# Loading the first gate block one step earlier, pairing rows of the narrow token blocks, other delays in a planner, and a last tile in halves

## The chip, the cores and the metric

One NeuronCore of a Trainium2 chip runs the whole program. The metric is the device time of one execution in microseconds; the median of three runs is given, and one further execution was taken with the profiler. TensorE (PE) does the matmuls, VectorE (DVE), ScalarE (ACT) and GpSimd (POOL) the element-wise work, SyncE (SP) issues the DMA transfers. Each engine works its own list of instructions in order, and waits where one of them needs another engine or a transfer.

## What is computed

One layer of an encoder: a normed input projection, differential attention and retention, and then the part that this change is in. 1024 prompt frames and 32 sample frames go through it together, 1056 tokens; the model has 1024 features, the feed-forward part 2816.

```python
def merge_and_tail(x, o_a, o_r, gate_a, gate_r, p, w_o, g_ffn, w_ff_gate, w_ff_up,
                   w_ff_down, g_ple, w_ple, w_ple_gate):
    mix = jax.nn.sigmoid(gate_a) * o_a + jax.nn.sigmoid(gate_r) * o_r
    x = x + mix @ w_o
    h = rmsnorm(x, g_ffn)
    x = x + (jax.nn.silu(h @ w_ff_gate) * (h @ w_ff_up)) @ w_ff_down
    gate = jax.nn.sigmoid(rmsnorm(x, g_ple) @ w_ple_gate)
    return x + gate * (p @ w_ple)
```

`rmsnorm` divides by the root of the mean square over the features and multiplies with a gain. The outputs are x for both sets of frames, and new keys, values and retention states.

## The kernel before

The matrices are fp32 and are multiplied as sums of 16-bit parts: every number is split into a high and a low half, and each product is three matmuls (L474, L475, L476: high-high, high-low, low-high). For that, each weight block comes by DMA into a stage buffer `st`, gets a scale, and is split into `w`.

Behind the attention stands one long stage, laid out by a planner (class `Flow`, L86). Each piece of work is a generator that yields what its next instruction costs and on which engine (`V`, `S`, `G`, `M` for VectorE, ScalarE, GpSimd, TensorE), waits for events, gets and puts buffers, or adds a `delay` to the time from which it may go on. The planner takes the piece that could start soonest by these estimates and writes out its instruction; so the estimates set the order of each engine's instructions, and where an operation may go on VectorE or GpSimd (`either_tt`, L1499) they choose the engine. Nothing of this runs on the chip: there only the resulting order exists.

The stage goes over the tokens in four blocks c0 to c3, of 352, 352, 176 and 176 tokens (`stream_bc`, L1796 on). For each block c and each of eight row tiles m (128 features), TensorE multiplies with w_o (24 matmuls to a tile). `residual(c)` (L1540) loads the block's x (`xf`, L1546), and for each m VectorE adds the product (L1553, the evacuation), SP stores the sum (L1556), ScalarE squares it (L1561), and VectorE adds the square to `acc` (L1564). TensorE then sums `acc` over the partitions (L1572, the norm sum of the block); VectorE, GpSimd and VectorE make of it `nbv`, `nbr` and `dg` (L1576, L1579, L1582), TensorE spreads `dg` (L1587), and VectorE scales the eight rows (L1591).

The gate and up projections follow in 22 weight blocks j. Two token blocks make a pair p: p = 0 is c0/c1, p = 1 is c2/c3; and (j, p) is gate block j on pair p, seven products of twelve matmuls. The pair's operands are not the rows themselves but rows and sums of rows: x1, x3, t1, t2, t4, x4 and t3. `sums(c, k)` (L1511) makes them by subtractions on VectorE or GpSimd, one row k at a time, and `parts16` (L1504) splits each into halves: ScalarE copies the high half (L1507), VectorE or GpSimd subtracts it to get the low half (L1501). x1, x3, t1 and x4 land in the tile called `mixs` in the trace, t2, t4 and t3 in `tT`.

`load_gu(j)` (L1613) brings a gate block: DMA into `st` (L1618, 1024 KB), two squares with a sum on ScalarE (L1630), their addition on VectorE (`wamh`, L1634), the sum over partitions on TensorE (L300, in `weight_scale`), a chain of tiny VectorE operations, and then seven splits shared by ScalarE, VectorE and GpSimd. The `delay` of L1635 tells the planner how long after `wamh` L300 is to be placed. Blocks 0 and 1 are asked for when the w_o loop reaches c = 1 (L1801), block 2 at c = 3, block 3 at (1, p = 0), and later blocks two steps ahead. There are two stage buffers.

The kernel's last stage (L1936 to L1960) goes over three blocks of 352 tokens and eight row tiles: 24 matmuls, a tanh on ScalarE (L1956), two VectorE operations (L1957, L1959) and a store (L1960).

Of the kernel before, what the change touches and what calls it, by code (L numbers as in the profile page):

```python
# [183 lines left out]
def kernel(  # L184
# [1278 lines left out]
    with ExitStack() as pc:  # L1463
# [18 lines left out]
        with ExitStack() as pw:  # L1482
# [20 lines left out]

            def parts16(key, out, src):  # L1504
                CW = WIDTH[2 * key[0]]
                yield S(CW, 0.05)
                nc.scalar.copy(out[0], src)  # L1507
                yield from either_tt(CW, out[1], src, out[0], ALU.subtract)
                yield ("set", ("o",) + key)

            def sums(c, k):  # L1511

                p, CW = c // 2, WIDTH[c]
                xa, xf, t = xfs[c - 1], xfs[c], tT[p]
                a1, a3, b2, b4 = xa[:, k], xa[:, HK + k], xf[:, k], xf[:, HK + k]
                cs = span(c)
                yield ("wait", ("o", p, "x1", k))
                yield from either_tt(CW, a1, b2, a1, ALU.subtract)
                flow.add(parts16((p, "t1", k), (xh1[:, k, 0, cs], xh1[:, k, 1, cs]), a1))

                if not p:
                    yield from either_tt(CW, b2, b4, b2, ALU.subtract)
# [4 lines left out]
                else:
                    yield ("wait", ("o", 0, "t2", k))
                    t2 = xfs[0][:, k, 0:CW]
                yield from either_tt(CW, t2, b4, a1, ALU.subtract)  # L1530
                flow.add(parts16((p, "t2", k), (t[:, T2, k, 0], t[:, T2, k, 1]), t2))
# [528 lines left out]
```

## Time and profile before

| | us |
|---|---|
| median of three runs | 1913.57 (1913.21 to 1913.68) |
| the profiled execution's own time | 1914.65 |
| its span, first to last instruction | 1912.8 |
| TensorE busy | 1860.5 (97%) |
| VectorE busy | 1503.2 (79%) |
| ScalarE busy | 1091.3 (57%) |
| GpSimd busy | 681.9 (36%) |

The mean granted clock of TensorE is 0.998 of full speed. The page gives these sums and the costliest groups of instructions; the views of the trace that are used below are the windows (how long each engine worked in a stretch, the granted clock there and the DMA engines' share), the waits (which instruction TensorE waited for, and how long), the timeline (single instructions, with the idle time ahead of them in brackets and what ended it), the instructions grouped by line and shape, and the DMA transfers with the time from issue to landing. Where neighbours of one line and shape follow each other, a timeline row holds several (x4), with the time from the first's start to the last's end. Matmuls overlap, so their spacing, not their length, is their price. The times of a trace count from its own start.

### The profile page before, as it was taken

The numbers are of one execution on the slowest core, as the hardware profiler recorded it, in microseconds if no ns is written. First come the engines' busy times: TensorE is split into PE (matmuls) and PEld (weight loads), VectorE is DVE, ScalarE is ACT, GpSimd is POOL, SyncE is SP. The second block draws the span as 40 slices with busy tenths as digits, with TensorE's granted clock in tenths as the row PEclk, the third lists the DMA queues.
The fourth block names the chain that finished last, engine by engine and source line by source line (L and its number), as shares of the span: only waits on it lengthen the run. The fifth ranks groups of instructions, "written<-read, shape, count | busy, mean of one in ns | idle before, by whom it ended". The sixth has DMA issues, their size and how long they took to land.

```text
span 1912.8 us, 38341 instructions
## 1 busy us (share of the span) xinstructions
PE 1860.5 (97%) x14183; PEld 1217.9 (64%) x14183; DVE 1503.2 (79%) x3955; ACT 1091.3 (57%) x2863; POOL 681.9 (36%) x1162
## 2 busy tenths in 40 slices
PE   7899999999999999999999998999999999999999
PEld 3556565555655566555556685777777776666665
DVE  7888888788787787777887589999999986654364
ACT  7777667677676776767656345655555552101132
POOL 3654444445444544544442067232232300000010
PEclk9999999999999999999999999999999999999999
DMA  5122112122021111211215610222111116112031
GB/s 192 71 72 78 60 32 82 36 57 81 26 68 58 50 64 34 80 59 30 85 34 191 222 65 29 101 83 87 65 59 63 50 53 262 62 61 79 11 133 50
DMA packets 71806, 146.91 MB, mean 77 GB/s; under 512 B 25249, under 2 KB 52001, under 8 KB 63682
## 3 DMA queue, kind: packets, MB, share of 16 engines
q1 hardware_dynamic: 71618, 144.46, 22.5%
q8 instruction: 111, 1.82, 0.4%
q14 instruction: 77, 0.63, 0.1%
HBM read 113.09 MB, written 31.34 MB: 76 GB/s over the span
## 4 chain that ended last, share of the span: by engine, by line
PE 70%; DVE 15%; POOL 6%; ACT 5%; issue 2%; DMA 1%; SPq 0%; POOLq 0%; ACTq 0%; DVEq 0%
PE ps L474 9%; PE ps L475 9%; PE ps L476 9%; PE pj L734 7%; PE pj L735 7%; PE pj L736 7%; PE ps L1478 4%; PE ps L1477 4%; PE ps L1476 4%; DVE nm L885 2%; ACT p L895 2%; DVE w L467 1%; POOL qkr L770 1%; PE sc L875 1%; PE sc L878 1%
## 5 line engine op out<-in xcount | busy, mean ns | idle before, releaser
L734 PE MATMUL pj<-w,xh 128*128 128x512 f16 x1024 | 388.9, 380 | 2.8 <-ACT w L465 2.8
L735 PE MATMUL pj<-w,xh 128*128 128x512 f16 x1024 | 389.0, 380 | 0.6 <-DVE w L467 0.6
L736 PE MATMUL pj<-w,xh 128*128 128x512 f16 x1024 | 389.0, 380 | 0.0
L475 PE MATMUL ps<-mixs,w 128*128 128x352 f16 (+1 forms) x960 | 260.6, 277 | 1.8 <-POOL mixs L1501 1.8
L474 PE MATMUL ps<-mixs,w 128*128 128x352 f16 (+1 forms) x960 | 260.7, 277 | 0.3 <-ACT pws L1354 0.3
L476 PE MATMUL ps<-mixs,w 128*128 128x352 f16 (+1 forms) x960 | 260.5, 277 | 0.0
L474 PEld LDWEIGHTS <-w 128*128 128x128 f16 x1728 | 169.7, 98 | 58.8 <-issue 5.1
L476 PEld LDWEIGHTS <-w 128*128 128x128 f16 x1728 | 169.5, 98 | 56.6 <-issue 5.6
L475 PEld LDWEIGHTS <-w 128*128 128x128 f16 x1728 | 169.5, 98 | 50.1 <-issue 1.3
L736 PEld LDWEIGHTS <-xh 128*128 128x128 f16 x1024 | 100.2, 98 | 122.3 <-issue 1.9
L1610 POOL TENSOR_TENSOR st<-st 128x512 f32<-128x512 f32 x66 | 86.2, 1305 | 250.7 <-DVE w L1605 186.6
L734 PEld LDWEIGHTS <-xh 128*128 128x128 f16 x1024 | 101.4, 99 | 76.7 <-issue 3.7
L735 PEld LDWEIGHTS <-xh 128*128 128x128 f16 x1024 | 100.2, 98 | 74.6 <-issue 3.7
L895 ACT ACTIVATE p<-sc,nb,scs 128x256 f32<-128x256 f32 (+7 forms) x128 | 106.6, 833 | 71.7 <-POOL nb L887 49.1
L475 PE MATMUL ps<-tT,w 128*128 128x352 f16 (+1 forms) x528 | 143.6, 277 | 3.5 <-DVE tT L1501 3.5
L476 PE MATMUL ps<-tT,w 128*128 128x352 f16 (+1 forms) x528 | 143.7, 277 | 0.0
L474 PE MATMUL ps<-tT,w 128*128 128x352 f16 (+1 forms) x528 | 143.6, 277 | 0.0
L1605 DVE SCALAR_TENSOR_TENSOR w<-st,gus,w 128x512 f16<-128x512 f32 x132 | 140.7, 1067 | 0.1
L885 DVE TENSOR_REDUCE nm<-sc 128x2 f32<-128x256 f32 (+6 forms) x112 | 102.9, 918 | 19.5 <-PE sc L878 18.3
L1478 PE MATMUL ps<-a,w 128*128 128x352 f16 x312 | 97.5, 313 | 0.5 <-DVE w L1696 0.5
L1476 PE MATMUL ps<-a,w 128*128 128x352 f16 x312 | 97.5, 313 | 0.0
L1477 PE MATMUL ps<-a,w 128*128 128x352 f16 x312 | 97.5, 312 | 0.0
(432 smaller groups left out, 4874.4 us busy)
## 6 DMA issues: line engine op xcount, KB each, us to landing
st<-in_win_dram SPq DMA_DIRECT2D x30, 1024.0 KB, 4.8
st<-in_wgu_dram SPq DMA_DIRECT2D x22, 1024.0 KB, 4.9
st<-in_wdn_dram SPq DMA_DIRECT2D x16, 704.0 KB, 4.5
out_dram<-kv SPq DMA_DIRECT2D x64, 128.0 KB, 1.7
a_d<-a SPq DMA_DIRECT2D x9, 528.0 KB, 2.6
b<-a_d SPq DMA_DIRECT2D x9, 528.0 KB, 7.1
mixs<-mix_d SPq DMA_DIRECT2D x8, 528.0 KB, 7.0
pw_d<-pws SPq DMA_DIRECT2D x12, 352.0 KB, 5.1
```

The costliest lines, as they stand in the source:

```text
L474: nc.tensor.matmul(out=ps, lhsT=wh, rhs=ah, start=first, stop=False)
L475: nc.tensor.matmul(out=ps, lhsT=wh, rhs=al, start=False, stop=False)
L476: nc.tensor.matmul(out=ps, lhsT=wl, rhs=ah, start=False, stop=last)
L734: nc.tensor.matmul(out=ps, lhsT=xhi, rhs=w[:, k, 0], start=(k == 0), stop=False)
L735: nc.tensor.matmul(out=ps, lhsT=xhi, rhs=w[:, k, 1], start=False, stop=False)
L736: nc.tensor.matmul(out=ps, lhsT=xh[:, k, 1, t0:t0 + P], rhs=w[:, k, 0], start=False, stop=(k == KD - 1))
L885: nc.vector.tensor_reduce(out=nm[0:R, mc], in_=pv, axis=AX.X, op=ALU.max, negate=True)
L895: nc.scalar.activation(pt[0:R, 0:NK], ps[0:R, p0:p0 + NK], AF.Exp, bias=nb[0:R, m:m + 1], scale=sc_ap[0:R], accum_out=Z[0:R, m:m + 1])
L1476: nc.tensor.matmul(out=ps, lhsT=wt[:, 0, j], rhs=a[:, 0, cs], start=(first and j == js[0]), stop=False)
L1477: nc.tensor.matmul(out=ps, lhsT=wt[:, 1, j], rhs=a[:, 0, cs], start=False, stop=False)
L1478: nc.tensor.matmul(out=ps, lhsT=wt[:, 2, j], rhs=a[:, 1, cs], start=False, stop=(last and j == js[-1]))
L1605: nc.vector.scalar_tensor_tensor(out=w[:, i, 1], in0=src, scalar=s, in1=w[:, i, 0], op0=ALU.mult, op1=ALU.subtract)
```

## The change

Four edits. (1) `load_gu(0)` is added when the w_o loop is at c = 0, and `load_gu(1)` at c = 1. (2) `ROWS = (1, 2)`: for the pair c2/c3, squares, `acc` additions, copies, subtractions and splits handle two rows of 176 in one instruction; the norm sum of c2 and c3 then takes eight small matmuls and no longer four. (3) The planner's delay behind `wamh` is 5.0 for the blocks 0 to 3 and stays 1.5 for the rest. (4) The last tile of the last stage is computed, evacuated and stored in two halves of 176 tokens.

```diff
@@ -1501,41 +1501,57 @@
                 ENG[g].tensor_tensor(out=out, in0=in0, in1=in1, op=op)
 
 
+
+            ROWS = (1, 2)
+
             def parts16(key, out, src):
-                CW = WIDTH[2 * key[0]]
-                yield S(CW, 0.05)
+                p, name, k = key
+                n, CW = ROWS[p], WIDTH[2 * p]
+                yield S(n * CW, 0.05)
                 nc.scalar.copy(out[0], src)
-                yield from either_tt(CW, out[1], src, out[0], ALU.subtract)
-                yield ("set", ("o",) + key)
+                yield from either_tt(n * CW, out[1], src, out[0], ALU.subtract)
+                for j in range(n):
+                    yield ("set", ("o", p, name, k + j))
 
             def sums(c, k):
 
                 p, CW = c // 2, WIDTH[c]
+                n = ROWS[p]
+                W = n * CW
+                lo, up = slice(k, k + n), slice(HK + k, HK + k + n)
                 xa, xf, t = xfs[c - 1], xfs[c], tT[p]
-                a1, a3, b2, b4 = xa[:, k], xa[:, HK + k], xf[:, k], xf[:, HK + k]
+                a1, a3, b2, b4 = xa[:, lo], xa[:, up], xf[:, lo], xf[:, up]
                 cs = span(c)
+
+                def row(ks):
+                    return xh1[:, ks, 0, cs], xh1[:, ks, 1, cs]
+
+                def tr(i):
+                    return t[:, i, lo, 0], t[:, i, lo, 1]
+
                 yield ("wait", ("o", p, "x1", k))
-                yield from either_tt(CW, a1, b2, a1, ALU.subtract)
-                flow.add(parts16((p, "t1", k), (xh1[:, k, 0, cs], xh1[:, k, 1, cs]), a1))
+                yield from either_tt(W, a1, b2, a1, ALU.subtract)
+                flow.add(parts16((p, "t1", k), row(lo), a1))
 
 ...
             def residual(c):
 
@@ -1546,7 +1562,8 @@
                 nc.sync.dma_start(out=xf, in_=xT[:, :, cs])
                 xfs.append(xf)
                 yield ("get", "acc")
-                acc = wkb.tile([P, CH], F32, tag="acc", name="acc")[:, 0:CW]
+                n = ROWS[p]
+                acc = wkb.tile([P, CH], F32, tag="acc", name="acc")[:, 0:n * CW]
                 for m in range(KD):
                     yield ("wait", ("wo", c, m))
                     yield V(CW, 1.0, 0.08)
@@ -1554,13 +1571,15 @@
                                                    op0=ALU.mult, op1=ALU.add)
                     yield ("put", "ps")
                     nc.sync.dma_start(out=x1_d[m, :, cs], in_=xf[:, m])
-                    if m:
+                    if m % n + 1 < n:
+                        continue
+                    if m >= n:
                         yield ("get", "sq")
-                    yield S(CW, 0.05)
-                    sq = wkb.tile([P, CH], F32, tag="sq", name="sq")[:, 0:CW] if m else acc
-                    nc.scalar.activation(sq, xf[:, m], AF.Square)
-                    if m:
-                        yield V(CW)
+                    yield S(n * CW, 0.05)
+                    sq = wkb.tile([P, CH], F32, tag="sq", name="sq")[:, 0:n * CW] if m >= n else acc
+                    nc.scalar.activation(sq.rearrange("p (a c) -> p a c", a=n), xf[:, m + 1 - n:m + 1], AF.Square)
+                    if m >= n:
+                        yield V(n * CW)
                         nc.vector.tensor_tensor(out=acc, in0=acc, in1=sq, op=ALU.add)
                         yield ("put", "sq")
                 yield ("get", "ss")
@@ -1569,8 +1588,9 @@
                 B = CW // 4
                 ps = pss.tile([P, 512], F32, tag="ss", name="ss")
                 for b in range(4):
-                    nc.tensor.matmul(out=ps[0:B, CW + b:CW + b + 1], lhsT=acc[:, b * B:(b + 1) * B], rhs=ones32[:, 0:1],
-                                     start=True, stop=True)
+                    for j in range(n):
+                        nc.tensor.matmul(out=ps[0:B, CW + b:CW + b + 1], lhsT=acc[:, j * CW + b * B:j * CW + (b + 1) * B],
+                                         rhs=ones32[:, 0:1], start=(j == 0), stop=(j + 1 == n))
                 yield V(4, 1.0, 0.1)
                 v = sm(4, "nbv")
                 nc.vector.tensor_scalar(out=v[0:B], in0=ps[0:B, CW:CW + 4], scalar1=_f(1.0 / D), scalar2=EPS, op0=ALU.mult, op1=ALU.add)
@@ -1590,8 +1610,12 @@
                     yield V(CW, 1.0, 0.08)
                     nc.vector.scalar_tensor_tensor(out=xf[:, k], in0=xf[:, k], scalar=gS[:, 1, k:k + 1], in1=ps[:, 0:CW],
                                                    op0=ALU.mult, op1=ALU.mult)
+                    k += 1 - n
+                    if k % n:
+                        continue
                     if not odd:
-                        flow.add(parts16((p, "x1" if k < HK else "x3", k % HK), (xh1[:, k, 0, cs], xh1[:, k, 1, cs]), xf[:, k]))
+                        ks = slice(k, k + n)
+                        flow.add(parts16((p, "x1" if k < HK else "x3", k % HK), (xh1[:, ks, 0, cs], xh1[:, ks, 1, cs]), xf[:, ks]))
                     elif k >= HK:
                         flow.add(sums(c, k - HK))
                 yield ("put", "ss")
@@ -1632,7 +1656,8 @@
                 yield V(1)
                 am = sm(1, "wamh", 3, BF16)
                 nc.vector.tensor_tensor(out=am, in0=am2[:, 0:1], in1=am2[:, 1:2], op=ALU.add)
-                yield ("delay", 1.5)
+
+                yield ("delay", 5.0 if j < 4 else 1.5)
                 s, d = yield from weight_scale(am, 1, 1, "gu", norm=True, total=True, at_bank=("ps", psb) if j < 4 else ("ss", pss))
 
                 yield V(1, 1.0, 0.2)
@@ -1798,9 +1823,8 @@
                 flow.add(residual(0), 0)
                 flow.add(residual(1), 0)
                 for c in range(NW):
-                    if c == 1:
-                        flow.add(load_gu(0), 2)
-                        flow.add(load_gu(1), 2)
+                    if c < 2:
+                        flow.add(load_gu(c), 2)
                     if c == 3:
                         flow.add(load_gu(2), 2)
                     if c in (1, 2):
@@ -1947,17 +1971,22 @@
                     norm2(wk, accs[c + 1], xts[c + 1], c + 1)
                 ms = slice(m % 4 * P, (m % 4 + 1) * P)
                 wt = wps[m // 4][0]
-                ps = bank()
-                for k in range(KD):
-                    xt = xts[c][k // 4][:, k % 4]
-                    mm3(ps, wt[:, k, 0, ms], wt[:, k, 1, ms], xt[:, 0], xt[:, 1], k == 0, k == KD - 1)
-                step()
-                th = wk.tile([P, CH], F32, tag="th", name="th")
-                nc.scalar.activation(th, ps, AF.Tanh, scale=hdp[:, m // 2:m // 2 + 1])
-                nc.vector.scalar_tensor_tensor(out=th, in0=th, scalar=1.0, in1=pws[:, m], op0=ALU.add, op1=ALU.mult)
-                yo = wk.tile([P, CH], F32, tag="yo", name="yo", bufs=3)
-                nc.vector.scalar_tensor_tensor(out=yo, in0=th, scalar=0.5, in1=x2[:, m, cs], op0=ALU.mult, op1=ALU.add)
-                nc.sync.dma_start(out=yT[m, :, cs], in_=yo)
+
+                n = 2 if (c, m) == (NCH - 1, KD - 1) else 1
+                for j in range(n):
+                    js = slice(j * CH // n, (j + 1) * CH // n)
+                    os = slice(cs.start + js.start, cs.start + js.stop)
+                    ps = bank()[:, 0:CH // n]
+                    for k in range(KD):
+                        xt = xts[c][k // 4][:, k % 4]
+                        mm3(ps, wt[:, k, 0, ms], wt[:, k, 1, ms], xt[:, 0, js], xt[:, 1, js], k == 0, k == KD - 1)
+                    step()
+                    th = wk.tile([P, CH], F32, tag="th", name="th")[:, js]
+                    nc.scalar.activation(th, ps, AF.Tanh, scale=hdp[:, m // 2:m // 2 + 1])
+                    nc.vector.scalar_tensor_tensor(out=th, in0=th, scalar=1.0, in1=pws[:, m, js], op0=ALU.add, op1=ALU.mult)
+                    yo = wk.tile([P, CH], F32, tag="yo", name="yo", bufs=3)[:, js]
+                    nc.vector.scalar_tensor_tensor(out=yo, in0=th, scalar=0.5, in1=x2[:, m, os], op0=ALU.mult, op1=ALU.add)
+                    nc.sync.dma_start(out=yT[m, :, os], in_=yo)
 
 
 # ---- launch: one core; inputs and outputs as the reference has them ----
```

What the change makes of the instructions' order. On SP, where the w_o loop begins, before (`xf` is x's load, `x_d` the store of the sum, `st` a weight block):

```order
L1546 DMA xf<-in_xT_dram 128x8x352 x2
L1556 DMA x_d<-xf 128x352 x2
L1546 DMA xf<-in_xT_dram 128x8x176
L1556 DMA x_d<-xf 128x352
L1618 DMA st<-in_wgu_dram 128x2048
```

The same place now, with the lines of the changed file:

```order
L1562 DMA xf<-in_xT_dram 128x8x352 x2
L1642 DMA st<-in_wgu_dram 128x2048
L1573 DMA x_d<-xf 128x352
L1562 DMA xf<-in_xT_dram 128x8x176 x2
L1573 DMA x_d<-xf 128x352
L1642 DMA st<-in_wgu_dram 128x2048
```

The first gate block's load moved ahead of the first stores, behind x's first two loads. On VectorE, in the same place, before:

```order
L461 SCALAR_TENSOR_TENSOR w<-st,wsk_16778,w 128x256 x4
L1553 SCALAR_TENSOR_TENSOR xf<-ps,o0d,xf 128x352
L461 SCALAR_TENSOR_TENSOR w<-st,wsk_16778,w 128x256 x3
L1553 SCALAR_TENSOR_TENSOR xf<-ps,o0d,xf 128x352
L461 SCALAR_TENSOR_TENSOR w<-st,wsk_16778,w 128x256
L1564 TENSOR_TENSOR acc<-acc,sq 128x352
```

And now:

```order
L461 SCALAR_TENSOR_TENSOR w<-st,wsk_16778,w 128x256 x4
L1570 SCALAR_TENSOR_TENSOR xf<-ps,o0d,xf 128x352
L461 SCALAR_TENSOR_TENSOR w<-st,wsk_16778,w 128x256 x3
L1570 SCALAR_TENSOR_TENSOR xf<-ps,o0d,xf 128x352
L1658 TENSOR_TENSOR wamh<-gam_16838 128x1
L461 SCALAR_TENSOR_TENSOR w<-st,wsk_16778,w 128x256
L1583 TENSOR_TENSOR acc<-acc,sq 128x352
```

`wamh` of gate block 0 came in ahead of w_o's last split; on TensorE its L300 stands behind the 96th of w_o's matmuls, where it stood behind the 264th. On TensorE, at the end of w_o on c3, where the first product of (0, p = 0) begins, before:

```order
L476 MATMUL ps<-mixs,w 128x176
L300 LDWEIGHTS cst_sb
L300 MATMUL mt<-wamh,cst_sb 128x1
L474 LDWEIGHTS w
L474 MATMUL ps<-mixs,w 128x352
```

24 matmuls of 352 columns later stood the norm sum of c3 (L1572). At that place now (L1592 is the norm sum):

```order
L476 MATMUL ps<-mixs,w 128x352
L1592 MATMUL ss<-cst_sb,acc 44x1 x8
L300 LDWEIGHTS cst_sb
L300 MATMUL mt<-wamh,cst_sb 128x1
L474 LDWEIGHTS w
L474 MATMUL ps<-mixs,w 128x352
```

Block 1's L300 moved from ahead of these 24 matmuls to behind the norm sum. In the same way block 3's L300, which stood inside (1, p = 1), now stands behind it and twelve matmuls of (2, p = 0); those of blocks 2 and 5 move by twelve matmuls. On VectorE, ahead of the norm sum of c3, before:

```order
L1564 TENSOR_TENSOR acc<-acc,sq 128x176
L1591 SCALAR_TENSOR_TENSOR xf<-xf,gS,ss 128x176
L1553 SCALAR_TENSOR_TENSOR xf<-ps,o1d,xf 128x176
L1591 SCALAR_TENSOR_TENSOR xf<-xf,gS,ss 128x176
L230 TENSOR_SCALAR guc<-mt 128x1
L1501 TENSOR_TENSOR mixs<-xf,mixs 128x176
L234 TENSOR_SCALAR gup_17938<-guc 128x1
L1501 TENSOR_TENSOR mixs<-xf,mixs 128x176
L1564 TENSOR_TENSOR acc<-acc,sq 128x176
```

And now:

```order
L1611 SCALAR_TENSOR_TENSOR xf<-xf,gS,ss 128x176 x3
L1570 SCALAR_TENSOR_TENSOR xf<-ps,o1d,xf 128x176
L1611 SCALAR_TENSOR_TENSOR xf<-xf,gS,ss 128x176
L1501 TENSOR_TENSOR tT_16818<-xf,tT_16818 128x352
L1583 TENSOR_TENSOR acc<-acc,sq 128x352
L1501 TENSOR_TENSOR tT_16818<-xf,tT_16818 128x352
L1501 TENSOR_TENSOR mixs<-xf,mixs 128x2x176 x2
```

The splits of x1 and x3 on c2 (`mixs`, 176) became pairs (2x176) and moved behind the last `acc` addition, which adds two rows. From VectorE's first subtraction (L1501) to that addition there are 36 instructions, before there were 43; up to the operands of (0, p = 1) 94, before 108. From about gate block 6 on, all engines have the same order as before, up to the last tile.

## Rows read from the trace of the kernel before

**Rows 1.** The page's first part: busy us, share of span, instructions.

```profile
PE 1860.5 (97%) x14183; PEld 1217.9 (64%) x14183; DVE 1503.2 (79%) x3955; ACT 1091.3 (57%) x2863; POOL 681.9 (36%) x1162
```

**Rows 2.** Windows: stretch, length; busy time (instructions) of PE, PEld, DVE, ACT, POOL; PEclk; DMA share; GB/s.

```profile
1054.40:1068.72 14.32, 14.32 (x97) 9.39 (x97) 8.79 (x25) 7.32 (x18) 0.00 (x0) 1.00 0.89 305
1054.40:1140.00 85.60, 85.60 (x748) 65.21 (x749) 57.22 (x115) 33.78 (x76) 29.02 (x27) 1.00 0.43 148
1140.00:1240.00 100.00, 84.35 (x728) 63.94 (x726) 98.28 (x216) 57.70 (x133) 55.37 (x57) 0.97 0.18 64
1148.00:1156.00 8.00, 5.97 (x36) 3.45 (x36) 8.00 (x24) 5.44 (x16) 6.77 (x8) 0.82 0.11 35
```

**Rows 3.** Waits of PE, 1085 to 1240: us in total, times, longest.

```profile
PE mt L300 <- DVE wamh L1634: 7.3, 5, 3.1
```

**Rows 4.** Timeline of PE: start, us, instruction, [idle before, releaser].

```profile
1148.03 0.16 PE L300 MATMUL mt<-wamh,cst_sb 128*128 128x1 bf16 x1 [3.07 <-DVE wamh L1634]
...
1155.16 0.46 PE L1572 MATMUL ss<-cst_sb,acc 128*44 128x1 f32 x8 [2.00 <-DVE gus L315]
...
1163.38 0.16 PE L300 MATMUL mt<-wamh,cst_sb 128*128 128x1 bf16 x1 [1.02 <-DVE wamh L1634]
...
1188.63 0.31 PE L475 MATMUL ps<-tT,w 128*128 128x176 f16 x1 [3.48 <-DVE tT L1501]
...
1193.04 0.24 PE L474 MATMUL ps<-mixs,w 128*128 128x176 f16 x1
...
1199.92 0.16 PE L300 MATMUL mt<-wamh,cst_sb 128*128 128x1 bf16 x1 [2.18 <-DVE wamh L1634]
```

**Rows 5.** Timeline of DVE, two places: w_o's splits, the last addition of c3.

```profile
1055.01 4.83 DVE L461 SCALAR_TENSOR_TENSOR w<-st,wsk,w 128x256 f16<-128x256 f32 x12
...
1153.62 1.40 DVE L1564 TENSOR_TENSOR acc<-acc,sq 128x176 f32<-128x176 f32 x1
```

**Rows 6.** Timeline of SP's queue: the loads of x for c0 and c1.

```profile
1054.83 1.85 SPq L1546 DMA_DIRECT2D xf<-in_xT_dram  x2
```

**Rows 7.** DMA issues of two short windows, c0's and c1's load: KB, us to landing.

```profile
xf<-in_xT_dram SPq DMA_DIRECT2D x1, 1408.0 KB, 9.6
...
xf<-in_xT_dram SPq DMA_DIRECT2D x1, 1408.0 KB, 12.2
```

**Rows 8.** Timeline of ACT: w_o's splits, and a gate block's squares.

```profile
1065.59 1.29 ACT L459 ACTIVATE w<-st,wsk 128x256 f16<-128x256 f32 x3
...
1087.84 1.04 ACT L1630 ACTIVATE w<-st 128x1024 bf16<-128x1024 f32 x1
...
1089.82 0.19 ACT L1630 ACTIVATION_READ_ACCUMULATOR w<-st 128x1 f32 x1
```

**Rows 9.** DVE by line and shape, 1131.8 to 1188.7: count | busy us, mean ns | idle.

```profile
L1501 DVE TENSOR_TENSOR tT<-xf,tT 128x352 f16<-128x352 f32 x8 | 5.5, 703 | 0.0
L1501 DVE TENSOR_TENSOR xf<-xf 128x352 f32<-128x352 f32 x6 | 5.5, 936 | 0.0
L1564 DVE TENSOR_TENSOR acc<-acc,sq 128x176 f32<-128x176 f32 x7 | 5.2, 739 | 0.0
L1501 DVE TENSOR_TENSOR mixs<-xf,mixs 128x176 f16<-128x176 f32 x6 | 4.5, 756 | 0.0
L1501 DVE TENSOR_TENSOR xf<-xf 128x176 f32<-128x176 f32 x4 | 2.9, 728 | 0.0
...
L1501 DVE TENSOR_TENSOR tT<-xf,tT 128x176 f16<-128x176 f32 x5 | 2.3, 484 | 0.0
...
L1501 DVE TENSOR_TENSOR mixs<-xf,mixs 128x352 f16<-128x352 f32 x1 | 1.2, 1168 | 0.0
```

**Rows 10.** Timeline of DVE: the last operation of the last tile.

```profile
1909.40 0.53 DVE L1959 SCALAR_TENSOR_TENSOR yo<-th,x 128x352 f32<-128x352 f32 x1
```

**Rows 11.** One line's instructions on DVE: duration ns min/median/max, first and last start, forms.

```profile
L1709 DVE SCALAR_TENSOR_TENSOR th<-th,snu x44: 328/432/835, 1173.4 to 1586.1; 128x352 f32<-128x352 f32 x22, 128x176 f32<-128x176 f32 x22
```

**Rows 12.** The page's DMA issues: KB each, median us to landing.

```profile
st<-in_wgu_dram SPq DMA_DIRECT2D x22, 1024.0 KB, 4.9
```

More of the change, by code (lines that the diff above doesn't have):

```diff
@@ L1527, in sums @@
                 else:
[L1528 to L1531, printed above, removed]
+                    for j in range(n):
+                        yield ("wait", ("o", 0, "t2", k + j))
+                    t2 = xfs[0][:, lo, 0:CW]
+                yield from either_tt(W, t2, b4, a1, ALU.subtract)
+                flow.add(parts16((p, "t2", k), tr(T2), t2))
                 yield ("wait", ("o", p, "x3", k))
-                yield from either_tt(CW, a3, t2, a3, ALU.subtract)
-                flow.add(parts16((p, "t4", k), (t[:, T4, k, 0], t[:, T4, k, 1]), a3))
+                yield from either_tt(W, a3, t2, a3, ALU.subtract)
+                flow.add(parts16((p, "t4", k), tr(T4), a3))
                 if p:
-                    flow.add(parts16((p, "x4", k), (xh1[:, HK + k, 0, cs], xh1[:, HK + k, 1, cs]), b4))
-                    yield from either_tt(CW, b2, b4, b2, ALU.subtract)
-                    flow.add(parts16((p, "t3", k), (t[:, T3, k, 0], t[:, T3, k, 1]), b2))
+                    flow.add(parts16((p, "x4", k), row(up), b4))
+                    yield from either_tt(W, b2, b4, b2, ALU.subtract)
+                    flow.add(parts16((p, "t3", k), tr(T3), b2))
             def residual(c):
@@ L1949 @@
                 wt = wps[m // 4][0]
-                ps = bank()
-                for k in range(KD):
-                    xt = xts[c][k // 4][:, k % 4]
-                    mm3(ps, wt[:, k, 0, ms], wt[:, k, 1, ms], xt[:, 0], xt[:, 1], k == 0, k == KD - 1)
-                step()
-                th = wk.tile([P, CH], F32, tag="th", name="th")
-                nc.scalar.activation(th, ps, AF.Tanh, scale=hdp[:, m // 2:m // 2 + 1])
-                nc.vector.scalar_tensor_tensor(out=th, in0=th, scalar=1.0, in1=pws[:, m], op0=ALU.add, op1=ALU.mult)
-                yo = wk.tile([P, CH], F32, tag="yo", name="yo", bufs=3)
-                nc.vector.scalar_tensor_tensor(out=yo, in0=th, scalar=0.5, in1=x2[:, m, cs], op0=ALU.mult, op1=ALU.add)
-                nc.sync.dma_start(out=yT[m, :, cs], in_=yo)
+                n = 2 if (c, m) == (NCH - 1, KD - 1) else 1
+                for j in range(n):
+                    js = slice(j * CH // n, (j + 1) * CH // n)
[11 more added lines that the diff above has]
+                    nc.sync.dma_start(out=yT[m, :, os], in_=yo)
 def _tables():
```

6 lines of the change are left out of this document (3 added, 3 removed).

## Prediction

> **What bounds the kernel now.** I read the page's busy shares first: TensorE works 97% of the span [rows 1]. So what can be won is the little time in which it stands still, and what can be lost is any new stand. The windows say where that is [rows 2]: from 1054.40, where w_o's matmuls begin, to 1140 it has no gap at all (85.60 of 85.60 us); from 1140 to 1240 it works 84.35 of 100 us, so 15.65 us stand open, and VectorE is busy 98.28 of these 100: VectorE paces there, and TensorE's waits are VectorE's queue. The waits of TensorE around that stretch name `wamh` five times, 7.3 us in all [rows 3]; this is the last VectorE step (L1634) before a gate block's scale goes through TensorE at L300. The timeline gives the places [rows 4]: 3.07 us at 1148.03 (block 1's scale), 2.00 at 1155.16 (norm sum of c3), 1.02 at 1163.38 (block 2's scale), 3.48 at 1188.63 (operands of block 0 on c2/c3), 2.18 at 1199.92 (block 3's scale).
>
> The clock is part of the price. From 1148 to 1156, right behind the 3.07 us wait, the granted clock is 0.82, while it is 1.00 where w_o runs [rows 2]: the lower of the two levels (1.2 instead of 2.4 GHz) took 0.18 x 8 = 1.4 us. The whole stretch from 1140 to 1240 has 0.97, that is 3 us, about two such falls, and it has two waits over 3 us. So I charge 1.4 us for a wait of over 3 us and nothing for one of about 2.
>
> **Part 1, gate block 0 asked for early.** Its load moves from the c == 1 step to c == 0. On SP it now stands directly behind the two `xf` loads. On TensorE its L300 stands behind 96 of w_o's matmuls and no longer behind 264; on ScalarE two squares go between w_o's last splits; on VectorE `wamh` goes ahead of w_o's last split and the evacuations behind it. When does TensorE ask, and when is it there?
> TensorE: 97 matmuls take 14.32 us from 1054.40 on, 0.148 each [rows 2]; the 96th ends at 1068.6.
> DMA: the stage buffer is the one that the first w_o block leaves. Its eighth split ends at 1055.01 + 8 x 0.40 = 1058.3 [rows 5]; from then on the transfer can be asked for. The two `xf` loads ahead, 1408 KB each, are issued from 1054.83 on, within 1.85 us [rows 6], the second 1.1 after the first; they take 9.6 and 12.2 us to land [rows 7], so they land at about 1064.4 and 1068.2, 3.8 us apart, with the DMA engines 0.89 busy [rows 2]. At that rate 1024 KB take 1024/1408 x 3.8 = 2.8 us: the block lands at about 1071.0.
> Then ScalarE squares the first half (1.04), does one w_o split (0.43), squares the second half (1.04) and reads the sum (0.19) [rows 8], and `wamh` follows: L300 can go at about 1071.0 + 2.7 = 1073.7. TensorE stands from 1068.6 to 1073.7, 5.1 us, and the clock falls: **+6.5 us**. At the window's mean of 305 GB/s [rows 2] the block takes 3.4 us, not 2.8, which makes 7.1; the bound below is that it doesn't queue at all, a rival below. Behind `wamh` VectorE's evacuations of w_o wait, behind the block x1's stores on SP's queue; TensorE wants neither before it goes on. Before the change block 0's L300 came without a wait. Nothing later takes the delay up: w_o runs without a gap to 1140, and the work that fills VectorE after that starts from products that are shifted with it.
>
> **Parts 2 and 3 up to the sum of c3** (times in before's frame, without part 1). `delay` 5.0 puts block 1's L300 behind the norm sum of c3. So the 3.07 us and their 1.4 go, and TensorE runs the 24 matmuls between the two places, from 1145.0 to about 1148.5, up to that sum. Now the accumulation of c3 is late instead. Before, its last add ran from 1153.62 for 1.40 us, to about 1155.0 [rows 5]. From its first subtraction at L1501 up to that add, VectorE now has 36 instructions where it had 43. By the mean of each form [rows 9]: out go 7 adds of 176 at 0.74, 3 `mixs` of 176 at 0.76, 2 `tT` of 352 at 0.70 and two tiny ones (5.2 + 2.3 + 1.4 + 0.1 = 9.0 us); in come 2 `xf` of 352 at 0.94, 2 `mixs` of 352 at 1.17 and 3 adds of 352. The stretch has no such add; the nearest rows are `tT` at 0.70 below and `mixs` at 1.17 above, and I take the 0.94 of `xf`, which also reads and writes fp32 (1.9 + 2.3 + 2.8 = 7.0). Net -2.0, bounds -1.3 and -2.7. The sum is free at about 1153.0; TensorE stands 4.5 us, and the clock falls. Against 1155.16 at full clock [rows 4] that leaves a gain of 0.7. Behind it the 1.02 us for block 2's scale goes, since its `wamh` now comes well ahead. So block 0 on c0/c1 ends about 1.7 us earlier.
>
> **Parts 2 and 3 on c2/c3.** Rows go two at a time there. TensorE wants the second pair of `t1` 19 matmuls into block 0 on c2/c3, and VectorE has to make it; before, its operands released TensorE last at 1188.63 [rows 4]. Over the whole piece, up to that point, VectorE has 94 instructions and had 108. By rows 9: adds -5.2 + 2.8; `mixs` of 176 -4.5, of 2x176 +2.8 (three at 0.94), of 352 +2.3; `tT` -2.4 (176) and -2.1 (352); `xf` of 176 -2.9, of 352 +2.8. Net -6.4; with each wide one that comes in at 1.17 it is -4.3, and VectorE may also have to wait for ScalarE's copies. So the pair is there between 1182.3 and 1185.5; I take 1184. TensorE, there since 1180, stands 4 us, loses 1.4 to the clock and has 65 matmuls of 176 left, which at half of 0.148 make 4.8: the block ends at 1190.3, where it was 1193.04 [rows 4]. That is -2.7 (bounds -1.2 and -4.5), and it contains the 1.7 above. Then block 1 on c2/c3 follows, and block 3's L300 now comes behind it and 12 more matmuls, later than its `wamh`: the 2.18 us go. Together **-4.9 us**, bounds -2.5 and -6.7. Blocks 2 and 5, whose places move by 12 matmuls, I set at nothing: what remains of the waits for scales, 7.3 less 3.07, 1.02 and 2.18 [rows 3, 4], is 1.0, and may double or go.
>
> Here the Trainium skill speaks against the merging. First the rows: VectorE's `xf` subtractions of 352 take 0.94 on average, those of 176 0.73 [rows 9], so twice the width costs 1.3 times the time. The Trainium skill's page "SBUF — State Buffer" (section "Who interferes with whom") says that a VectorE instruction with two SBUF inputs and a GpSimd instruction that reads SBUF exclude each other, and that the one which comes second is blocked for the whole of the other. By it a wide operation waits out a wide one of GpSimd, whose operations get wider too, and the sum would go towards the second rival's time.
>
> **Part 4, the last tile in two halves.** 48 matmuls of 176 cost what 24 of 352 did. Behind the last one, ScalarE's tanh and two VectorE operations of 0.53 each [rows 10] now work on half the columns. Such an operation took 0.33 at the least where half-wide ones ran [rows 11]: 2 x 0.2 us, and for the tanh and the half-sized store some 0.1 each: **-0.6 us**, bounds -0.3 and -0.9.
>
> **The sum.** +6.5 - 4.9 - 0.6 = +1.0 us on the profiled execution's own 1914.65, so 1915.7. That execution lies 1.08 above the median of 1913.57; against the median the forecast is **1914.6 us**. A measurement of this kernel can tell 0.2%, 3.8 us, from no change: faster means below 1909.7, slower above 1917.4.
>
> **Rivals.**
> *The early load needn't wait its turn (faster).* If the block doesn't stand behind `xf`, it needs what such a block needs in the median of all 22, 4.9 us [rows 12]: 1058.3 + 4.9 = 1063.2. ScalarE's squares are done by 1066, and TensorE never stands. From a landing before 1066 on the wait is nil: 1914.6 - 6.5 = 1908.1. A landing at 1068 leaves 2 us and no fall of the clock, 1910. Against it: the second `xf` landed 3.8 us after the first though issued 1.1 after it, so the queue worked them off one behind the other [rows 7]. For it: nothing but the median.
> *Wide operations eat the saving (slower).* Merged rows only pay while an operation of 352 costs less than two of 176. The one `mixs` of 352 took 1.17, two of 176 take 1.51 [rows 9], and GpSimd gets wide ones on the same tiles. If the wide ones average 1.4, as long as the add at 1153.62 took with 176 columns [rows 5], nine of them cost 0.4 to 0.5 more each, the pair comes at 1188, and the -2.7 turns to +1.2: the saving is gone and the new waits keep their falls of the clock. 1914.6 + 3.9 = 1918.5. It decides from about 1.35 us for a wide operation on.
> *Scales late again (near no change).* If block 3's `wamh` is late after all, 2.2 us come back: 1916.8. Another 1 to 2 us are possible where block 1's split weights, whose scale is now 5 us later, are wanted.
>
> **How the numbers follow.** The sum with its smaller variants (early wait 4.5 to 5.7, gate stretch within its bounds, a scale late): 0.63, times from 1911 to 1917.5. The early load without a wait or with a short one: 0.20, from 1905.5 to 1910.5. Wide operations eat the saving: 0.17, from 1917 to 1921. The range that leaves 2 in 10 out is 1907.5 to 1919. Faster: most of the second case and a little of the first, 0.24. Slower: most of the third and a little of the first, 0.22. Within: 0.54.
>
> **What would show it.** The changed kernel's TensorE must show one wait of 4.5 to 6 us at its first gate scale, behind w_o's 96th matmul, released by `wamh`, with a granted clock near 0.8 behind it; the first gate block landing 12 to 13 us after 1058; no wait at block 1's scale; one of about 4 us at the norm sum of c3; one of 3 to 5 us at a `mixs` of 176 in block 0 on c2/c3; none at block 3's scale; and the last store some 0.6 us sooner behind the last matmul. I am wrong if TensorE runs through the first scale, or if VectorE's mean for `xf` or `mixs` of 352 lies above 1.35 us.

## The result, and the profile after

The changed kernel takes 1918.61 us in the median of ten runs (1916.85 to 1920.16); the kernel before takes 1913.37 on the same chip. The ratio is 1.0026, with a 95% interval of 1.0018 to 1.0034: 5.2 us slower, more than the 0.2% that can be told from no change. The forecast was 1914.6 with "no change" as the likeliest; the time lies inside the range, 1907.5 to 1919, but only 0.4 us below its upper end. The profiled execution took 1918.57, its span is 1916.8, the mean granted clock 0.995.

The waits of TensorE from 1050 to 1260 (us in total, times, longest), where [rows 3] had five for `wamh`:

```profile
PE ps L475 <- DVE mixs L1501: 6.8, 1, 6.8
PE mt L300 <- DVE wamh L1658: 5.7, 1, 5.7
PE ss L1592 <- DVE acc L1583: 4.0, 1, 4.0
PE ss L1607 <- DVE dg L1602: 1.1, 1, 1.1
```

There are fewer waits, and they are longer: three over 3 us, before there were two. Their places, in TensorE's timeline (L1592 is the norm sum, L1658 `wamh`; the row at 1193.63 is the second pair of `t1`, that is its rows 2 and 3, which are made in one instruction now):

```profile
1053.52 0.31 PE L474 MATMUL ps<-mixs,w 128*128 128x352 f16 x1 [0.33 <-ACT pws L1354]
...
1067.69 0.31 PE L476 MATMUL ps<-mixs,w 128*128 128x352 f16 x1
1073.67 0.16 PE L300 MATMUL mt<-wamh,cst_sb 128*128 128x1 bf16 x1 [5.67 <-DVE wamh L1658]
...
1074.53 0.50 PE L474 MATMUL ps<-mixs,w 128*128 128x352 f16 x1
1074.83 0.50 PE L475 MATMUL ps<-mixs,w 128*128 128x352 f16 x1
...
1159.87 0.42 PE L1592 MATMUL ss<-cst_sb,acc 128*44 128x1 f32 x4 [3.99 <-DVE acc L1583]
...
1193.63 0.30 PE L475 MATMUL ps<-mixs,w 128*128 128x176 f16 x1 [6.75 <-DVE mixs L1501]
...
1201.34 0.24 PE L474 MATMUL ps<-mixs,w 128*128 128x176 f16 x1
...
1209.50 0.17 PE L300 MATMUL mt<-wamh,cst_sb 128*128 128x1 bf16 x1
```

The first gate scale stands behind w_o's 96th matmul (the row at 1067.69) and waits 5.67 us; the next matmuls are 0.30 apart. Block 3's scale at 1209.50 has no bracket: it doesn't wait any more. ScalarE's first square (L1654) tells when the block was there:

```profile
1070.06 1.06 ACT L1654 ACTIVATE w<-st 128x1024 bf16<-128x1024 f32 x1 [4.71 <-DMA st<-in_wgu_dram]
```

SP had asked for it at 1057.4, so it took 12.6 us to land, behind both loads of x; in this kernel's frame the forecast's 1071.0 is 1070.1. The windows behind the three long waits, and the stretch that [rows 2] showed (length; busy of PE, PEld, DVE, ACT, POOL; PEclk; DMA share; GB/s):

```profile
1073.67:1081.67 8.00, 8.00 (x46) 4.83 (x46) 7.18 (x18) 4.46 (x8) 1.94 (x2) 0.82 0.70 227
...
1159.87:1167.87 8.00, 8.00 (x47) 4.94 (x48) 6.64 (x18) 4.21 (x8) 5.25 (x4) 0.66 0.01 2
...
1193.63:1197.63 4.00, 4.00 (x28) 4.00 (x28) 3.96 (x7) 1.03 (x3) 1.75 (x2) 0.50 0.00 0
1197.63:1201.63 4.00, 4.00 (x43) 4.00 (x42) 4.00 (x12) 2.06 (x5) 0.04 (x1) 0.77 0.00 0
...
1140.00:1240.00 100.00, 88.19 (x768) 68.32 (x767) 95.65 (x191) 56.26 (x118) 60.08 (x50) 0.91 0.16 55
```

The lower clock costs (1 - 0.82) x 8 = 1.4 us behind the first wait, 0.34 x 8 = 2.7 behind the second and 0.50 x 4 + 0.23 x 4 = 2.9 behind the third. In the profile before, the same reckoning gave 1.4 at its first long wait.

So where did the time come from? Both kernels counted from their first w_o matmul (1054.40 and 1053.52; the 0.9 between them lies ahead of the change, and in the other runs' traces this matmul starts anywhere from 1053.2 to 1054.4):

| place | before | after | later by | forecast |
|---|---|---|---|---|
| norm sum of c0 | 1090.20 | 1096.57 | 7.2 | 6.5 |
| norm sum of c3, behind its wait | 1155.16 | 1159.87 | 5.6 | 4.5 |
| (0, c2/c3) begins | 1179.51 | 1185.28 | 6.6 | 4.8 |
| (1, c2/c3) begins | 1193.04 | 1201.34 | 9.2 | 3.8 |
| the next 352-column product, block 2 | 1201.77 | 1207.71 | 6.8 | 1.6 |
| two blocks on (their scales' waits gone too) | 1241.03 | 1245.59 | 5.4 | 1.6 |
| end of the span | 1912.8 | 1916.8 | 4.9 | 1.0 |

The early question (gate block 0 asked for one step sooner) cost about what it was to cost. Between the norm sum of c3 and the end of (0, c2/c3) the gain that was forecast didn't come.

### The profile page after: what moved, and what is told of

It is laid out like the page before. It is cut to its first block, busy times and chain, and to the rows that moved or that the text cites. A ratio compares the mean times of both kernels' runs of the same rounds, so it can differ in the third digit from the quotient of the medians.

```text
span 1916.8 us, 38364 instructions
## 1 busy us (share of the span) xinstructions
PE 1863.0 (97%) x14223; PEld 1221.7 (64%) x14223; DVE 1497.3 (78%) x3941; ACT 1087.9 (57%) x2842; POOL 676.9 (35%) x1148
## 4 chain that ended last, share of the span: by engine, by line
PE 72%; DVE 12%; POOL 7%; ACT 5%; issue 2%; DMA 2%; SPq 0%; POOLq 0%; ACTq 0%; DVEq 0%
PE ps L474 9%; PE ps L475 9%; PE ps L476 9%; PE pj L734 7%; PE pj L736 7%; PE pj L735 7%; PE ps L1478 4%; PE ps L1477 4%; PE ps L1476 4%; ACT p L895 2%; DVE nm L885 2%; DVE w L467 1%; POOL qkr L770 1%; PE sc L875 1%; PE sc L878 1%
```

## The experiments

Each was timed in five rounds against the kernel before on the same chip; the ratio is to that kernel, with its 95% interval, and the diffs are against the changed kernel unless something else is said.

| run | us | before, same chip | ratio |
|---|---|---|---|
| gate block 0 asked for late again | 1911.02 | 1913.57 | 0.9984 (0.9975 to 0.9993) |
| before, with the early question alone | 1925.25 | 1913.57 | 1.0059 (1.0047 to 1.0072) |
| single rows | 1917.63 | 1913.57 | 1.0020 (1.0011 to 1.0029) |
| early load, later scale | 1910.77 | 1913.57 | 0.9986 (0.9977 to 0.9994) |
| delays and tail only | 1910.89 | 1914.20 | 0.9984 (0.9975 to 0.9993) |
| pairing and tail only | 1910.50 | 1914.20 | 0.9982 (0.9973 to 0.9991) |
| no operand subtractions on GpSimd | 1925.80 | 1914.20 | 1.0060 (1.0048 to 1.0073) |
| norm sum of c3 later | 1919.32 | 1914.20 | 1.0027 (1.0017 to 1.0038) |
| block 0 ahead of c1's x | 1912.37 | 1913.84 | 0.9994 (0.9985 to 1.0003) |
| before, with the halved tail alone | 1913.32 | 1913.84 | 0.9998 (0.9989 to 1.0006) |
| early load, later scale, short delays | 1910.35 | 1913.84 | 0.9983 (0.9974 to 0.9992) |

### The early question

Undone:

```diff
-                    if c < 2:
-                        flow.add(load_gu(c), 2)
+                    if c == 1:
+                        flow.add(load_gu(0), 2)
+                        flow.add(load_gu(1), 2)
```

> The changed kernel with gate block 0 asked for at c == 1 again, together with block 1; paired rows, delays and the halved last tile stay. Theory (the early question makes TensorE stand 5.7 us behind w_o's 96th matmul and lose 1.4 us of clock, and gives nothing back): that wait is gone and the time falls by 7, to about 1911.4 (1910 to 1913). Rival (the early question also relieves VectorE in front of the gate blocks, since block 0's splits are done sooner): the waits at the norm sum of c3 (3.99) and at t1's second pair (6.75) grow by 2 to 4 us together, and the time is 1914 to 1916.

1911.02: 0.42% less than the changed kernel, 8 us. The waits at the norm sum and at t1's pair are what they were in the changed kernel:

```profile
PE ps L475 <- DVE mixs L1501: 6.7, 1, 6.7
PE ss L1592 <- DVE acc L1583: 4.0, 1, 4.0
```

So the early question gave nothing back behind its own wait; the rival, that it relieves VectorE later, falls. Done alone, in the kernel before (the same lines the other way round):

> The kernel before with gate block 0 asked for at c == 0 alone; the short delay then puts its L300 behind 72 of w_o's matmuls, 24 sooner than in the changed kernel. Theory: the block can't be there sooner, so TensorE stands 24 x 0.149 = 3.6 us longer than the 5.67 us there, some 9.2, and loses 1.4 us of clock: 1913.4 + 10.6 = 1924 (1922 to 1926). Rival (it relieves VectorE later): under 1920.

1925.25, 11.7 above before; its wait for `wamh` behind 72 of w_o's matmuls is 8.94 us. The block comes when it comes: a scale placed 24 matmuls sooner waits 3.3 us longer.

Is it the place in the queue that makes the block late? An exchange on SP's queue tells:

```diff
@@ residual(c), ahead of the load of xf
+                if c == 1:
+                    yield ("wait", "gu0")
@@ load_gu(j), behind its dma_start
+                if j == 0:
+                    yield ("set", "gu0")
```

> The changed kernel with one exchange on SP's queue: block 0's load goes ahead of the xf load of c1, behind that of c0 alone; all engines' orders stay. Theory (the block was late because 1408 KB of xf stood ahead of it in the queue): it lands some 3.5 us sooner, at about 1066.5 in the changed kernel's frame, wamh is there at about 1069.6, TensorE comes at 1068.0 and stands 1.6 us (0.5 to 2.5) in place of 5.67 and keeps its clock: 1918.6 - 4.1 - 1.4 = 1913.1 (1912 to 1914.5). Rival (the block's landing is set by the DMA engines' load and not by its place): as the changed kernel, 1917.5 to 1919.5.

1912.37, as the theory said. The block lands 8.7 us after its issue at 1057.1, at 1065.8, and in TensorE's timeline the wait is short and the matmuls behind it are 0.15 apart:

```profile
1069.44 0.16 PE L300 MATMUL mt<-wamh,cst_sb 128*128 128x1 bf16 x1 [1.75 <-DVE wamh L1662]
1069.46 0.31 PE L474 MATMUL ps<-mixs,w 128*128 128x352 f16 x1
1069.61 0.31 PE L475 MATMUL ps<-mixs,w 128*128 128x352 f16 x1
```

TensorE, VectorE, ScalarE and GpSimd have the orders of the changed kernel, so 6 us of its loss hang on SP's queue, and in the main on the 1408 KB of x that stood ahead of the block. A smaller thing moved with it: the loads of x for c2 and c3, issued from 1064.83 on in the changed kernel while the block was still landing, now come from 1069.72 on, when it is there. What they added to the 12.6 us isn't separated; the forecast of the landing, 1070.1, was met without them. The cheaper remedy leaves the queue alone and moves the scale:

```diff
-                yield ("delay", 5.0 if j < 4 else 1.5)
+                yield ("delay", 16.0 if j == 0 else 5.0 if j < 4 else 1.5)
```

> The changed kernel with a planner's delay of 16 behind the wamh of block 0 only: its L300 stands behind 168 of w_o's matmuls, where TensorE comes at about 1078.6, five us after wamh; the early load and squares stay. Theory: no wait and no fall of the clock at the first scale, the rest as in the changed kernel: 1918.6 - 7.1 = 1911.5 (1910 to 1913). Rival (the early load itself costs, by queueing in front of x1's stores or by splits among w_o's evacuations): 1914 to 1917.

1910.77. At 1078.60 TensorE runs through the first scale, and the rest is as it was: 4.0 at the norm sum, 6.7 at t1's pair.

### Pairing, delays and the tail

Single rows (`ROWS = (1, 1)`) in the changed kernel:

> The changed kernel with single rows on c2/c3 (ROWS of 1 and 1). Theory A (pairing rows saves VectorE some 3 us before t1's second pair): without it the waits at the norm sum and at t1 grow, 1920 to 1922. Theory B (pairing saves nothing, because GpSimd's wider operations hold VectorE up elsewhere by as much): within 1 us of the changed kernel, 1917.5 to 1919.5. Theory C (pairing is what makes t1 late): 1914 to 1916.

1917.63: theory B, pairing saves no time. But the waits are others. In this kernel they are (1055 to 1240):

```profile
PE ss L1592 <- DVE acc L1583: 5.5, 1, 5.5
PE mt L300 <- DVE wamh L1658: 4.9, 1, 4.9
PE ps L474 <- ACT w L1626: 2.8, 1, 2.8
PE ps L476 <- DVE w L1629: 2.5, 1, 2.5
```

At t1 there is none; TensorE now waits for block 1's split weights at (1, c0/c1), whose scale the delay moved back, and comes to (0, c2/c3) at 1194.0 when the operands are there. With pairs it comes at 1185.3 and waits to 1193.6. So pairs don't bring VectorE through any sooner: its last operand subtraction (L1501) starts at 1193.50 with pairs and at 1190.97 with single rows, GpSimd's last at 1194.25 and 1198.47.

The same without the early question, once with the delays and once with the pairing (the diffs are the lines above; the latter has `delay` 1.5 throughout):

> The changed kernel with gate block 0 asked for at c == 1 and with single rows: of the four edits only the delays and the halved last tile stay. Theory (pairing gives nothing in time, since GpSimd holds VectorE up elsewhere by as much): as e1_late_ask, 1911.0, within 1.2 us. Rival (pairing gave 2 us that the early question hid): 1912.5 to 1914.

> The changed kernel with gate block 0 asked for at c == 1 and the delay of 1.5 for all blocks: of the four edits only pairing and the halved last tile stay. Theory (the delays take away the waits at the scales, some 2.2 us in (1, c2/c3) and 0.9 at block 5, while VectorE sets the rest): 3 us slower than e1_late_ask, 1913 to 1915. Rival (VectorE sets everything up to block 6, delays don't matter): 1910.5 to 1912.

1910.89 and 1910.50, and both edits together 1911.02. In the first, theory as expected; in the second the rival, which said that the delays don't matter beside pairing. Either edit alone, with the tail, is worth 3 to 4 us, and the second adds nothing to the first. In the run with pairing and tail the scales of the blocks 3 and 5 don't wait either, though their delay is 1.5 as before, where they waited 2.18 and 0.91; the waits for the blocks 1 and 2 are still there, 2.50 and 1.02. The tail by itself:

> The kernel before with the last tile in halves, nothing else. Theory: 0.6 to 0.8 us less than before, since the last tanh, two VectorE operations and store work on half. Rival (twice the small matmuls and weight loads eat it): no change.

1913.32 against 1913.84, 0.5 less; the interval (0.9989 to 1.0006) doesn't exclude "no change". The traces show it more sharply: from the last matmul's start to the end of the span it is 1912.8 - 1907.9 = 4.9 us before, and 1916.8 - 1912.6 = 4.2 in the changed kernel, where the last operations are these:

```profile
1913.31 0.34 DVE L1986 SCALAR_TENSOR_TENSOR th<-th,pws 128x176 f32<-128x176 f32 x1 [1.10 <-ACT th L1985]
1913.69 0.34 DVE L1988 SCALAR_TENSOR_TENSOR yo<-th,x 128x176 f32<-128x176 f32 x1
```

### VectorE and GpSimd

What did pairing do to VectorE? By line and shape, in the changed kernel from 1137 to 1193.7 (count | busy us, mean ns), the lines that answer to [rows 9] and some others:

```profile
L1629 DVE SCALAR_TENSOR_TENSOR w<-st,gus,w 128x512 f16<-128x512 f32 x9 | 9.5, 1079 | 0.0
...
L1501 DVE TENSOR_TENSOR xf<-xf 128x352 f32<-128x352 f32 x9 | 5.5, 630 | 0.0
L1501 DVE TENSOR_TENSOR mixs<-xf,mixs 128x352 f16<-128x352 f32 x6 | 4.4, 741 | 0.0
L1501 DVE TENSOR_TENSOR tT<-xf,tT 128x352 f16<-128x352 f32 x6 | 4.2, 698 | 0.0
L1583 DVE TENSOR_TENSOR acc<-acc,sq 128x352 f32<-128x352 f32 x4 | 4.1, 1017 | 0.0
L1602 DVE TENSOR_TENSOR dg<-cst_sb,nbr 44x176 f32<-44x176 f32 x2 | 3.7, 1862 | 0.9 <-POOL nbr L1599 0.9
L1658 DVE TENSOR_TENSOR wamh<-gam 128x1 bf16<-128x1 f32 x2 | 3.0, 1478 | 0.0
...
L1739 DVE SCALAR_TENSOR_TENSOR a<-a,th 128x352 f16<-128x352 f16 x2 | 2.3, 1202 | 0.0
...
L1734 DVE SCALAR_TENSOR_TENSOR th<-th,snu 128x352 f32<-128x352 f32 x1 | 1.2, 1250 | 0.0
```

The same lines before, from 1131.8 to 1188.7, where [rows 9] doesn't show them:

```profile
L1605 DVE SCALAR_TENSOR_TENSOR w<-st,gus,w 128x512 f16<-128x512 f32 x9 | 8.2, 923 | 0.0
...
L1582 DVE TENSOR_TENSOR dg<-cst_sb,nbr 44x176 f32<-44x176 f32 x2 | 2.4, 1191 | 0.9 <-POOL nbr L1579 0.9
...
L1714 DVE SCALAR_TENSOR_TENSOR a<-a,th 128x352 f16<-128x352 f16 x2 | 1.7, 875 | 0.0
...
L1634 DVE TENSOR_TENSOR wamh<-gam 128x1 bf16<-128x1 f32 x2 | 1.4, 682 | 0.0
...
L1709 DVE SCALAR_TENSOR_TENSOR th<-th,snu 128x352 f32<-128x352 f32 x1 | 0.8, 835 | 0.0
```

The wide subtractions of `xf` and `mixs` became cheaper, not dearer (`xf` 0.63, before 0.94; `mixs` 0.74, before 1.17), and those of `tT` cost what they did. Others became dearer: the nine splits, `wamh`, an addition of a single column, `dg`, and the operations on `th` and `a`, which work on finished products of the gate blocks. What stands beside `dg` and `wamh` on GpSimd (timelines of both engines, VectorE's first):

```profile
1144.52 3.41 DVE L1602 TENSOR_TENSOR dg<-cst_sb,nbr 44x176 f32<-44x176 f32 x1 [0.90 <-POOL nbr L1599]
...
1161.59 2.10 DVE L1658 TENSOR_TENSOR wamh<-gam 128x1 bf16<-128x1 f32 x1
```

```profile
1144.46 1.65 POOL L1501 TENSOR_TENSOR tT<-xf,tT 128x352 f16<-128x352 f32 x2
1146.08 1.65 POOL L1501 TENSOR_TENSOR mixs<-xf,mixs 128x352 f16<-128x352 f32 x2
...
1161.44 1.00 POOL L1599 TENSOR_TENSOR nbr<-nbv,neghalf 44x4 f32<-44x4 f32 x1 [2.10 <-DVE nbv L1596]
1162.42 1.26 POOL L1634 TENSOR_TENSOR w<-st 128x512 f32<-128x512 f32 x1
```

`dg` begins as GpSimd begins four operations in a row and ends about as the last of them ends; `wamh` spans two. To see whether that is cause or chance, GpSimd got no operand subtraction at all (in the kernel with the later scale):

```diff
-                g = yield either(V(n), G(n))
-                ENG[g].tensor_tensor(out=out, in0=in0, in1=in1, op=op)
+                yield V(n)
+                nc.vector.tensor_tensor(out=out, in0=in0, in1=in1, op=op)
```

> As e6_scale_later, but all subtractions of the operands (L1501) on VectorE, none on GpSimd; 27 to 30 wide ones move. Theory (a GpSimd operation of 1.0 to 1.2 us holds up whatever two-input operation VectorE has next, wide or tiny, about as long as VectorE would need for two of its own): VectorE's wide subtractions take 0.51, wamh 0.15, dg 0.3, and its time above the undisturbed one, 22 us in the changed kernel, falls below 10; VectorE's queue ends about as before or earlier, the time is 1907 to 1912. Rival (VectorE is simply short of time; GpSimd's help is worth what it does): 30 x 0.44 = 13 us come onto VectorE, the second t1 pair is late by 8 or more, 1918 or above.

More operations moved than the 27 to 30 expected: 43 of the 66 that stand at L1501 were GpSimd's. Half of the theory holds. VectorE by line and shape, from 1130 to 1190, where GpSimd has only ten operations left:

```profile
L1501 DVE TENSOR_TENSOR tT<-xf,tT 128x352 f16<-128x352 f32 x18 | 14.8, 829 | 0.0
L1501 DVE TENSOR_TENSOR xf<-xf 128x352 f32<-128x352 f32 x22 | 11.2, 512 | 0.0
...
L1501 DVE TENSOR_TENSOR mixs<-xf,mixs 128x352 f16<-128x352 f32 x16 | 7.9, 511 | 0.0
...
L1602 DVE TENSOR_TENSOR dg<-cst_sb,nbr 44x176 f32<-44x176 f32 x2 | 0.7, 330 | 0.9 <-POOL nbr L1599 0.9
...
L1658 DVE TENSOR_TENSOR wamh<-gam 128x1 bf16<-128x1 f32 x2 | 0.2, 152 | 0.0
```

`dg` takes 0.33 and not 1.86, `wamh` 0.15 and not 1.48: they waited for GpSimd. This agrees with the rule that the prediction cites from the Trainium skill's page "SBUF — State Buffer", section "Who interferes with whom". The mean of `tT`, 0.83, hides one of 6.23 beside the five GpSimd operations that did remain there (VectorE's row first); the other seventeen take 0.51.

```profile
1150.78 6.23 DVE L1501 TENSOR_TENSOR tT<-xf,tT 128x352 f16<-128x352 f32 x1
```

```profile
1150.52 1.20 POOL L1599 TENSOR_TENSOR nbr<-nbv,neghalf 44x4 f32<-44x4 f32 x1 [12.12 <-DVE nbv L1596]
1151.70 2.49 POOL L1634 TENSOR_TENSOR w<-st 128x512 f32<-128x512 f32 x2
1154.15 2.48 POOL L1634 TENSOR_TENSOR st<-st 128x512 f32<-128x512 f32 x2
```

But the time is 1925.80, and there the rival was right: with all the subtractions on VectorE the kernel is 15 us slower than the one it was made from. TensorE now waits 7.2 us for the next scale and in seven other places. How much of this is VectorE's added work, and how much that one stop, which stood ahead of c3's `dg`, and the new order that the planner laid out, the run doesn't separate.

The last question was whether the waits at the norm sum and at t1 add up or are one and the same (again in the kernel with the later scale):

```diff
-                yield ("delay", 2.0 if c + 1 < NW else 0.5)
+                yield ("delay", 2.0 if c + 1 < NW else 7.0)
                 yield M(0.3)
```

> As e6_scale_later, but with the norm sum of c3 placed 48 matmuls later on TensorE, and block 1's scale 48 matmuls ahead of it. Theory (VectorE's queue sets when the c2/c3 operands are there, so a wait removed at the sum comes back at t1): no wait at the sum, some 4 to 5 us more at t1's pair, one fall of the clock less; 1909 to 1911. Rival (the waits are independent): 4.0 + 1.4 us less, 1905 to 1906.

Neither: 1919.32. The wait at the sum is gone, but its successors come late: TensorE stands 6.8 us for `dg` (L1602), and at t1's second pair 8.6 for ScalarE's copy and 1.0 more for the subtraction behind it, where it stood 6.7. The planner laid out everything behind the sum anew, so the run doesn't answer the question; it suggests that the norm chain of c3, not only VectorE's amount of work, stands ahead of the c2/c3 operands.

Last, the early load with a later scale and the short delays, since with pairing the scales of the blocks 3 and 5 didn't wait under short delays either:

```diff
-                yield ("delay", 5.0 if j < 4 else 1.5)
+                yield ("delay", 16.0 if j == 0 else 1.5)
```

> The changed kernel with a delay of 16 for block 0 and 1.5 for all others: early load, pairing and halved tail, L300 of block 0 behind 168 of w_o's matmuls and the other scales where the kernel before had them. Theory (no wait at the first scale; delays and pairing don't add up, and the early splits give nothing): as e8_late_d15 and e6_scale_later, 3 us below the kernel before, 1910 to 1911.5. Rival (the early splits relieve VectorE a little): 1908 to 1909.5.

1910.35: as the theory said, 3.5 below before, and the lowest time of all. It beats both kernels, but four others lie within 0.7 us of it.

## Why the prediction was half right

*The early question* was right by mechanism and nearly by size: +6.5 forecast, 7.2 in the trace (5.67 of wait, 1.4 of clock, and a little), 8.0 and 7.7 in the two runs without the wait (0.42% and 0.40%, each ratio good to about 0.1%). Its steps hold: the queue (12.6 us to landing with both loads of x ahead, 8.7 with one), the two squares, no slack later. The first rival, a load that needn't queue, falls.

*The norm sum of c3.* The wait there is 3.99, 4.5 was forecast, and `acc` is done 1.7 us sooner relative to the shift, 2.0 was forecast. Wrong was the clock: 2.7 us, not 1.4.

*The second t1 pair* is the step that failed. In before's frame (1193.63 + 0.9 - 7.2) it comes at 1187.3; the forecast took 1184 and, at the latest, 1185.5. The sum behind that counted 14 instructions less and priced each by its own mean, as if the time that VectorE loses to GpSimd belonged to the form that shows it. The runs show that it doesn't. The forms that the sum counted took 27.1 us before and 16.2 up to the pair after (`xf` 5.5, `mixs` 4.4, `acc` 3.3, `tT` 3.0; the list's first `acc` and last `tT` lie outside this piece), 10.9 less and not 6.4. But splits, `dg`, `wamh`, `th` and `a`, which it left as they were, took 18.1 before and 24.8 after: 6.7 more. (Neighbouring rows overlap a little, so these sums come to more than the busy time.) From its first subtraction to the pair VectorE was busy 53.3 us after, 55.9 before: of 6.4 us that should have gone, 2.6 went, and idle gaps took 1.5 of these. Part of the wait may also be the planner's order, which no run tried by itself: TensorE took the pair's high half at 1186.64 without a wait, so its copy was done, GpSimd stood idle from 1187.38 to 1189.00, and the low half stood in VectorE's queue until 1192.43. Then the clock came on top, 2.9 us in place of 1.4. The two together, 3.3 + 1.5, are what (1, c2/c3) begins later than the forecast, apart from the early question's 0.7.

*The second rival* has the right time for a wrong reason. It gave 1918.5 and put the pair at 1188; its mechanism, wide operations of over 1.35 us, isn't there: their means lie from 0.63 to 1.02. What it left out is that whichever two-input operation stands next pays. So its time was met by luck, and that the main sum's range holds the time is luck in part as well: the sum said +1.0, and +5.2 came.

*The scales.* Block 3's wait went, 2.18 us, as forecast; that the longer delay is what removed it isn't shown, since with pairing it went under the short delay too. The two late ones that were set at nothing (0.16 and 0.91 before) went as well. *The tail* gave 0.7, 0.6 was forecast.

Together the gate stretch gave 1.8 us (7.2 less the 5.4 of the table) in place of 4.9; with the 0.7 that the early question cost more, this is 3.8 of the 4.0 us between 1914.6 and 1918.6. What the runs without the early question say fits: 1911 is 2.5 below before, 1.8 from the stretch and 0.7 from the tail.

## What to carry to other kernels

A scale or weight that is asked for early is only early if nothing big stands ahead of it on its queue: work out its landing from the transfers ahead, then place the instruction that needs it behind that point on the engine that mustn't stand. Where two engines hold each other up, don't price a removed instruction by the mean of its own form: part of that mean is the other engine's time, and the next instruction inherits it. And two edits that each gain alone need not add up in the same stretch: here the delays with the tail gave 3.3 us, the pairing with the tail 3.7, and all three together 2.5. Try each alone.

## What the runs showed of the hardware that was not expected

The fall of TensorE's clock has no fixed price. Behind a wait of 5.67 us, where matmuls of 352 columns followed, it cost 1.4 us (granted clock 0.82 over 8 us); behind 3.99 us, where eight small matmuls of one column came first, 2.7 (0.66 over 8 us); behind 6.75 us, where matmuls of 176 columns followed, 2.9 (0.50 and 0.77 over 4 us each). After 1.75 us, and after 2.18 before, it stayed at 1.00. Wait and following work differ together in these three places, so which of them sets the price isn't shown.

A VectorE operation can be held up by several GpSimd operations in a row: `dg`, 0.33 us undisturbed, took 3.41 beside four of them, and `wamh`, 0.15 undisturbed, took 2.10 beside two, and a subtraction for `tT`, 0.51 undisturbed, 6.23 beside five. The page of the Trainium skill that the prediction cites speaks of one whole instruction; here the wait went on through the next ones.
